# Two of the four weight units of an output projection split earlier, into small tiles

## The chip, the core and the metric

The kernel runs on one core of a Trainium2 chip. The metric is the time of one execution on the device in microseconds (us); three runs of the kernel before gave 1076.39, 1076.57 and 1077.71 us, with a median of 1076.57. One more execution was taken with the hardware profiler, and every row below comes from that one.

## What is computed

One layer of a hybrid block on 528 tokens (16 meta tokens and 512 of the input) of width 1024. The change touches the mixing of the two branches and the projection behind it:

```python
mixed = (jax.nn.sigmoid(ga) * (o_a @ w_branch_rnn[l])
         + jax.nn.sigmoid(gb) * (o_b @ w_branch_ret[l]))
h = h + mixed @ w_out[l]
xn = rms_norm(h, norm_ffn_g[l])
up = causal_dwconv(xn @ w_up[l], ffn_conv_w[l], ffn_conv_b[l])
```

Here `ga` and `gb` are columns of the normed input times `w_in`, `o_a` is the output of the recurrent branch (1280 wide) and `o_b` that of the retention branch (2048 wide). `w_out` is 1024 x 1024. The result is in float32 and the kernel keeps near that precision: each float32 operand is split into two float16 forms, a high one (scaled and rounded) and a low one (the rest), and each product is three matmuls (high by high, high by low, low by high: `SPLIT`).

## The kernel before, in words

**Weights.** All weights come from HBM as float32 in *units* of at most 1 MB, listed once in the order of use (`unit`, line 110; the list is built in lines 114 to 181). `unit_load` (line 186) takes the next unit of the list, claims one of the **two** raw buffers (`wraw`, `bufs=2`, tile `raw`) and issues its load on SP's queue; it returns the unit's *steps*. A step calls `split` (line 90): ScalarE (ACT) makes the high form (line 91), then VectorE (DVE) the low form from the raw data and the high form (line 92). The forms stand in tiles `wt` of the pool `wsp`, ten buffers of 2 x 1024 float16 columns. A raw buffer is free for the next load only when the last low form of its unit is made.

A plain unit has two steps of up to 1024 columns and takes two `wt` tiles. A *fast* unit (`fast_steps`, line 212; a Strassen-like scheme with seven products in place of eight) has five steps and takes four tiles: **cut 1** (512 columns: B11), **cut 2** (1024: B21, B22), three sums on VectorE over the raw data (lines 231 to 233), **cut 3** (1024: T1, T3) and **cut 4** (1024: T4, T2). Cut 3 reads what line 231 writes, cut 4 what lines 232 and 233 write.

**Order.** Steps and loads go strictly in the order of the list. `get(u)` emits all steps up to unit `u`; `tick()` emits one step ahead, as long as the `wt` tiles of the units from the current one to that step's are at most `ahead`. In this part of the program the instructions of each engine are then put into a fixed order when the program is built, by a list scheduler; on the chip each engine runs its own list in that order, and an instruction that waits holds back all that stand behind it.

**The stretch of the change.** Block `i` (`gate_b(i)`, line 1038, i = 0 to 3) makes columns 256 i to 256 i + 255 of the mixed result: a gate unit of `w_in` (*gate unit i*, `u_gb[i]`) and two units of `w_branch_ret` (*branch units 2 i and 2 i + 1*, `u_bb`). Each runs `fast_products` (line 768) on TensorE (PE), here in seven steps: B11 into the bank `pa` (ACT copies it to `kept`), T3 into `pe`, T2 added in `pa` (copied to `kept` again), B21 into `pb`, T1 added in `pa` (copied to `last`), B22 added in `pa` (read by `func`), T4 added in `pe`. `pa` is one PSUM bank, so T2, T1 and B22 can start only when ACT has made the copy ahead of them:

```python
        product(pa, "T2", "F6")
        keep(kept[:, h1], pa)
        yield
        pb = bank("pb")
        product(pb, "B21", "A12", True)
        nc.vector.tensor_tensor(g0[:, h0], pb[:, :257], kept[:, h0], op=ALU.add)
        yield
        product(pa, "T1", "F5")
        keep(last[:, h0], pa)
```

In between, `branch` (line 991, tile `pm`) multiplies the ten tiles `oa` of the first branch with a unit of `w_branch_rnn`; the eighth and last of these stands between blocks 1 and 2. Each `oa` is a *piece*, a buffer of the pool `pieces` (46 buffers, line 57), and is read for the last time there.

After block 3 `out_proj(i)` (line 1104) multiplies the mixed tiles `mx` with the four units of `w_out` (*output units 0 to 3*, `u_out`, line 172, two tiles `wt` each), and after each of its four row tiles come a norm (lines 317 to 331), transposes (line 337, `ptr`) and splits (`x2h`, `x2l`). The last norm runs beside the first three half products of the up projection (line 383).

Of the kernel before, what the change touches and what calls it, by code (L numbers as in the profile page):

```python
# [9 lines left out]
F16 = mybir.dt.float16  # L10
# [4 lines left out]
P = 128  # L15
# [14 lines left out]
SW = 2.0 ** 8  # L30
# [20 lines left out]
def hybrid_block_kernel(ctx, tc, x, meta, norm_mix_g, w_in, conv_w, conv_b, rg_a_w, rg_a_b,  # L51
# [5 lines left out]
    pieces = ctx.enter_context(tc.tile_pool(name="pieces", bufs=46))  # L57
    wraw = ctx.enter_context(tc.tile_pool(name="wraw", bufs=2))
    wsp = ctx.enter_context(tc.tile_pool(name="wsp", bufs=10))
# [24 lines left out]
    def piece(shape, dtype, name):  # L84
        return pieces.tile(shape, dtype, name=name, tag="s")
# [4 lines left out]
    def split(hi, lo, src, s):  # L90
        nc.scalar.activation(hi, src, AF.Copy, scale=s)  # L91
        nc.vector.scalar_tensor_tensor(lo, src, s, hi, op0=ALU.mult, op1=ALU.subtract)  # L92
# [3 lines left out]
    def load(dst, src):  # L96

        if last_load[0] is None:
            last_load[0] = nc.sync.dma_start(dst, src)
        else:  # L100
            with tc.issue_after(last_load[0].ins):
                last_load[0] = nc.sync.dma_start(dst, src)


    def kmaj(w, k0, nk, c0, ncol):
        return w[k0 * P:(k0 + nk) * P, c0:c0 + ncol].rearrange("(k p) c -> p k c", p=P)

    units = []

    def unit(nk, ncol, parts, fast=False):  # L110
        units.append((nk, ncol, parts, fast))
        return len(units) - 1

    o_ur, o_ug, o_q, o_k, o_v, o_gr, o_ga, o_gb = 0, 1280, 2560, 3584, 4608, 6656, 8704, 9728
# [1 line left out]
    for n in range(2):  # L116
        u_ur.append((unit(8, P, [(0, 0, kmaj(w_in, 0, 8, o_ur + P * n, P))]), 0))
    for i in range(1, 5):
        u = unit(8, 256, [(0, 0, kmaj(w_in, 0, 8, o_ur + 256 * i, 256))])
        u_ur += [(u, 0), (u, P)]  # L120
    u_ug = [unit(8, 256, [(0, 0, kmaj(w_in, 0, 8, o_ug + 256 * i, 256))]) for i in range(5)]
    u_q, u_k = [], []
    for h in range(HEADS):
# [21 lines left out]
    def add_ba():  # L145
        u_ba.append(unit(10, P, [(0, 0, kmaj(w_brnn, 0, 10, P * len(u_ba), P))]))

    def add_gate(us, o):
        us.append(unit(8, 256, [(0, 0, kmaj(w_in, 0, 8, o + 256 * len(us), 256))], fast=True))

    def add_bb():
        i = len(u_bb) // 2
        for g in range(2):
            rows = w_bret[8 * P * g:8 * P * (g + 1)].rearrange("(i j p) c -> p j i c", i=4, j=2)
            u_bb.append(unit(8, 256, [(4 * j, 0, rows[:, j, :, 256 * i:256 * i + 256]) for j in range(2)], fast=True))
# [6 lines left out]
    add_gate(u_ga, o_ga)  # L162
    add_ba()
    add_ba()
    for i in range(4):
        add_gate(u_gb, o_gb)
        add_bb()
        if i == 0:
            add_gate(u_ga, o_ga)
        if i < 2:  # L170
            add_ba()
    u_out = [unit(2, 1024, [(0, 0, kmaj(w_out, 2 * a, 2, 0, 1024))]) for a in range(4)]
    u_up = []
    for j in range(12):
        u_up.append([unit(8, 256, [(0, 0, kmaj(w_up, 0, 8, a * DFF + 256 * j, 256))]) for a in range(2)])
# [7 lines left out]
    wviews = []  # L183
    loaded = []

    def unit_load(cuts=1):

        nk, ncol, parts, fast = units[len(loaded)]
        raw = wraw.tile([P, 2048], F32, name="raw")
        n = nk * ncol  # L190
        rv = raw[:, :n].rearrange("p (k c) -> p k c", k=nk)
        for k0, c0, ap in parts:
            load(rv[:, k0:k0 + ap.shape[1], c0:c0 + ap.shape[2]], ap)
        loaded.append(len(loaded))
        if fast:
            return fast_steps(rv, nk // 2, ncol // 2)
        hk = nk // 2
        hn = hk * ncol
        tiles = []

        def step(i, c):
            def run():
                if c == 0:
                    tiles.append(wsp.tile([P, 2, 1024], F16, name="wt"))
                sl = slice(c * hn // cuts, (c + 1) * hn // cuts)
                split(tiles[i][:, 0, sl], tiles[i][:, 1, sl], raw[:, i * hn:(i + 1) * hn][:, sl], SW)
            return run

        wviews.append(lambda a, k, c0, m: tiles[k // hk][:, a, k % hk * ncol + c0:k % hk * ncol + c0 + m])
        return [step(i, c) for i in range(2) for c in range(cuts)]  # L210

    def fast_steps(rv, bk, bc):


        tiles = []
        top, low = slice(0, bk), slice(bk, 2 * bk)
        left, right = slice(0, bc), slice(bc, 2 * bc)

        def cut(rows, cols):
            def run():  # L220
                t = wsp.tile([P, 2, 1024], F16, name="wt")
                src = rv[:, rows, cols]
                n = bk * src.shape[2]
                tv = [t[:, a, :n].rearrange("p (k c) -> p k c", k=bk) for a in range(2)]
                tiles.append(tv)
                split(tv[0], tv[1], src, SW)
            return run

        def sums():
            pair = rv[:, top].rearrange("p k (h c) -> p h k c", h=2)  # L230
            nc.vector.tensor_tensor(pair, pair, rv[:, :, right].rearrange("p (h k) c -> p h k c", h=2), op=ALU.add)  # L231
            nc.vector.tensor_tensor(rv[:, low, right], rv[:, top, left], rv[:, low, right], op=ALU.add)
            nc.vector.tensor_tensor(rv[:, low, left], rv[:, low, left], rv[:, low, right], op=ALU.add)

        at = {"B11": (0, 0), "B21": (1, 0), "B22": (1, bc), "T1": (2, 0), "T3": (2, bc), "T4": (3, 0), "T2": (3, bc)}

        def form(nm, a, k):
            i, c0 = at[nm]
            return tiles[i][a][:, k, c0:c0 + bc]

        wviews.append(form)
        return [cut(top, left), cut(low, slice(0, 2 * bc)), sums,
                cut(top, slice(0, 2 * bc)), cut(low, slice(0, 2 * bc))]
# [4 lines left out]
    current = [0]  # L248

    def unit_tiles(u):  # L250
        return 4 if units[u][3] else 2

    def emit_step():
        u, run = steps[done[0]]
        while len(loaded) < min(u + 2, len(units)):
            queue(unit_load())
        run()
        done[0] += 1
# [4 lines left out]
    def get(u):  # L263
        current[0] = max(current[0], u)
        while len(loaded) <= u:
            queue(unit_load())
        while done[0] < len(steps) and steps[done[0]][0] <= u:
            emit_step()
        return wviews[u]

    def tick(n=1):

        for _ in range(n):
            if done[0] == len(steps):
                if len(loaded) == len(units):
                    return
                queue(unit_load())
            u = steps[done[0]][0]
            if sum(unit_tiles(i) for i in range(current[0], u + 1)) > ahead[0]:
                return  # L280
            emit_step()
# [340 lines left out]
    for n in range(NR):  # L622
        ps = acc("ps")
        u, col = u_ug[n // 2], (n % 2) * P
# [49 lines left out]
    for h in range(HEADS):  # L674
        t = [[piece([P, 2, T], F16, f"qk{h}{i}{m}") for m in range(2)] for i in range(2)]
# [207 lines left out]
    def gate_unit(h, i):  # L883
        ot = oraw[h]

        def finish(j, g):
            nc.vector.tensor_mul(ot[2 * i + j], g[:, :TQ], ot[2 * i + j])
            if j == 0:
                ob_forms(h, i, ot[2 * i], ot[2 * i + 1])

        return fast_products([get(u_gr[h][i])], x_forms, gate_func(AF.Silu), finish)
# [130 lines left out]
    for i in range(2):  # L1022
        run = gate_unit(3, i)
# [48 lines left out]
    wo = [get(u) for u in u_out]  # L1072
# [196 lines left out]
    def combine(pd, left, right):  # L1269

        e1 = work.tile([P, 512], F32, name="e1", tag="w")
        nc.scalar.activation(e1, pd["P1"], AF.Copy)
        yield
        s2 = total(pd["P6"], e1, "s2")
        yield
        s3 = total(pd["P7"], s2, "s3")
        add(1, left, s3, un)
        yield
        add(1, left, pd["P4"], un)
        yield  # L1280
        s7 = total(pd["P5"], s3, "s7")
        add(1, right, s7, -un)
        s4 = total(pd["P5"], s2, "s4")
        add(0, right, s4, -un)
        yield
        add(0, left, e1, un)
        add(0, left, pd["P2"], un)
        yield
        add(0, right, pd["P3"], -un)
        yield  # L1290
# [9 lines left out]
    for q in range(6):  # L1300
        get(u_dn[q])
        run = combine(pd, slice(0, 256), slice(512, 768))
# [22 lines left out]
    run = combine(pd, slice(256, 512), slice(768, 1024))  # L1325
# [78 lines left out]
```

## Time and profile before

| | us |
|---|---|
| median of three runs | 1076.57 |
| the profiled execution | 1076.25 |
| its span, first to last instruction | 1074.5 |
| TensorE busy in the span (matmuls) | 1055.9 (98%) |
| VectorE busy | 839.0 (78%) |
| ScalarE busy | 567.5 (53%) |
| GpSimd busy | 6.8 (1%) |
| 16 DMA engines, HBM read | 108.57 MB |

Times in the rows below count from the span's start. The granted clock of TensorE is at 90% or more in each of the page's 40 slices, 0.999 in the mean. Busy time of TensorE is the union of its matmuls' spans, which overlap: a matmul of 257 columns has a span of 0.27 us, but the next starts 0.11 us later.

### The profile page before, as it was taken

What the parts mean: (1) busy time and instruction counts of PE and PEld (TensorE: products, weight loads), DVE (VectorE), ACT (ScalarE), POOL (GpSimd) and SP (SyncE); (2) the same over time, 40 slices, a digit from 0 to 9 for tenths busy, and PEclk for the clock granted to TensorE, in tenths of its full rate; (3) what the DMA queues carried; (4) which work ended last, traced back from release to release, by engine and by line L of the source; (5) the groups of instructions that cost most, each with busy time, mean ns of one, the idle gap of its engine ahead of it and who ended that gap; (6) DMA issues with size and microseconds to landing.
All of it is one profiled execution on the core that took longest, in us unless ns stands there. A gap on an engine that the chain in (4) does not pass through costs nothing.

```text
span 1074.5 us, 20950 instructions
## 1 busy us (share of the span) xinstructions
PE 1055.9 (98%) x9037; PEld 855.1 (80%) x9037; DVE 839.0 (78%) x1219; ACT 567.5 (53%) x847; POOL 6.8 (1%) x20
## 2 busy tenths in 40 slices
PE   8999999999999999999999999999999999999997
PEld 5888888865684858888888885588888888888885
DVE  6875799998786969878697785578767777888875
ACT  6558954435564747566454453365444544454442
POOL 2000000000000000000000000000000000000000
PEclk9999999999999999999999999999999999999999
DMA  7432243431212212423333355143232323113322
GB/s 220 133 117 80 80 138 119 157 120 40 80 41 72 88 62 65 128 89 119 103 104 119 118 200 174 38 159 118 79 118 80 119 79 118 41 60 126 111 79 79
DMA packets 108027, 112.00 MB, mean 104 GB/s; under 512 B 5546, under 2 KB 99472, under 8 KB 107936
## 3 DMA queue, kind: packets, MB, share of 16 engines
q1 hardware_dynamic: 107504, 110.27, 31.4%
q8 instruction: 70, 1.15, 0.4%
q10 hardware_dynamic: 144, 0.26, 0.1%
q0 software_dynamic: 288, 0.14, 0.1%
q14 instruction: 21, 0.17, 0.0%
HBM read 108.57 MB, written 2.10 MB: 103 GB/s over the span
## 4 chain that ended last, share of the span: by engine, by line
PE 75%; DVE 14%; ACT 8%; issue 2%; DMA 1%; SPq 0%; ACTq 0%; DVEq 0%
PE ps L370 33%; PE P L1240 9%; PE pa L776 9%; PE ps L839 4%; PE pm L370 4%; PE ps L1112 4%; PE pe L776 4%; DVE wt L92 3%; PE ps L383 3%; PE pb L776 2%; ACT wt L91 2%; PE ps L861 1%; DVE rnn L575 1%; DVE raw L231 1%; ACT L627 1%
## 5 line engine op out<-in xcount | busy, mean ns | idle before, releaser
L370 PEld LDWEIGHTS <-wt 128*128 128x128 f16 x4224 | 410.5, 97 | 63.7 <-DVE t L667 1.4
L92 DVE SCALAR_TENSOR_TENSOR wt<-raw,wt 128x1024 f16<-128x1024 f32 (+2 forms) x270 | 296.6, 1111 | 71.5 <-ACT wt L91 69.5
L91 ACT ACTIVATE wt<-raw 128x1024 f16<-128x1024 f32 (+2 forms) x270 | 256.4, 965 | 161.1 <-PE ps L370 28.3
L776 PEld LDWEIGHTS <-wt 128*128 128x128 f16 x2016 | 195.0, 97 | 36.0 <-issue 8.8
L370 PE MATMUL ps<-x2h,wt 128*128 128x258 f16 x1440 | 218.8, 273 | 0.0
L370 PE MATMUL ps<-xh,wt 128*128 128x257 f16 (+2 forms) x1056 | 163.8, 275 | 1.1 <-DVE t L667 1.1
L370 PE MATMUL ps<-x2l,wt 128*128 128x258 f16 x720 | 137.7, 272 | 0.0
L1197 DVE SCALAR_TENSOR_TENSOR cv<-ps,vt,cv 128x512 f32<-128x512 f32 x96 | 71.9, 749 | 54.7 <-ACT cv L1195 53.4
L370 PE MATMUL ps<-xl,wt 128*128 128x257 f16 (+2 forms) x528 | 102.2, 275 | 0.0
L1240 PE MATMUL P<-wt,act 128*128 128x256 f16 x792 | 88.3, 273 | 0.0
L1240 PEld LDWEIGHTS <-act 128*128 128x128 f16 x792 | 77.5, 98 | 9.0
L839 PE MATMUL ps<-wt,xh 128*128 128x512 f16 x256 | 76.4, 379 | 1.2 <-DVE v L92 1.0
L776 PE MATMUL pa<-xs,wt 128*128 128x257 f16 x576 | 71.6, 273 | 4.8 <-ACT kept L781 4.5
L1195 ACT ACTIVATE cv<-ps,vt,vt 128x512 f32<-128x512 f32 x48 | 37.1, 773 | 56.8 <-PE ps L370 52.2
L370 PE MATMUL pm<-oa,wt 128*128 128x257 f16 x480 | 55.4, 274 | 0.0
L839 PEld LDWEIGHTS <-xh 128*128 128x128 f16 x256 | 24.8, 98 | 30.9 <-issue 2.9
L839 PE MATMUL ps<-wt,xl 128*128 128x512 f16 x128 | 48.5, 379 | 0.0
L776 PE MATMUL pa<-ob,wt 128*128 128x257 f16 x384 | 45.7, 274 | 0.6 <-ACT last L781 0.5
L1112 PE MATMUL ps<-wt,mx 128*128 128x512 f16 x192 | 44.3, 379 | 0.0
L231 DVE TENSOR_TENSOR raw<-raw 128x1024 f32<-128x1024 f32 x35 | 42.7, 1220 | 0.6
L1112 PEld LDWEIGHTS <-mx 128*128 128x128 f16 x192 | 17.6, 98 | 18.5
L861 PE MATMUL ps<-sc,v 128*128 128x257 f16 (+4 forms) x384 | 32.1, 236 | 0.0
(250 smaller groups left out, 1273.5 us busy)
## 6 DMA issues: line engine op xcount, KB each, us to landing
raw<-in_w_in SPq DMA_DIRECT2D x41, 1024.0 KB, 4.8
raw<-in_w_up SPq DMA_DIRECT2D x24, 1024.0 KB, 5.0
raw<-in_w_down SPq DMA_DIRECT2D x48, 256.0 KB, 3.4
raw<-in_w_branch_ret SPq DMA_DIRECT2D x16, 512.0 KB, 4.3
raw<-in_w_branch_rnn SPq DMA_DIRECT2D x8, 640.0 KB, 4.2
raw<-in_w_out SPq DMA_DIRECT2D x4, 1024.0 KB, 4.9
xin<-in_x SPq DMA_DIRECT2D x4, 512.0 KB, 4.9
h<-in_x SPq DMA_DIRECT2D x4, 512.0 KB, 4.3
```

What stands on the lines that cost most here:

```text
L91: nc.scalar.activation(hi, src, AF.Copy, scale=s)
L92: nc.vector.scalar_tensor_tensor(lo, src, s, hi, op0=ALU.mult, op1=ALU.subtract)
L231: nc.vector.tensor_tensor(pair, pair, rv[:, :, right].rearrange("p (h k) c -> p h k c", h=2), op=ALU.add)
L370: nc.tensor.matmul(ps[:, hf, :n], w(aw, k, col, P), src(ax, k, c0, n), start=k == 0 and (aw, ax) == (0, 0), stop=k == nk - 1 and aw == 1)
L383: mm = nc.tensor.matmul(ps[:, hf, :n], w(aw, k, col, P), src(ax, k, c0, n), start=k == 0 and (aw, ax) == (0, 0), stop=k == KD - 1 and aw == 1)
L776: nc.tensor.matmul(ps[:, :257], ws[k // 4](wf, aw, k % 4), src(xf_, ax, k), start=first and k == 0 and (aw, ax) == (0, 0), stop=k == last_ ...
L839: nc.tensor.matmul(pb, xf(ax, k, XF + j0, nb), w(aw, k % 4, 0, 512), start=i == 0, stop=i == 23)
L861: nc.tensor.matmul(ps[:, hf, s0 - lo_i:257], vt[b][:, va, d * P:(d + 1) * P], st[SCP[b][0]][:, sa, o:o + hi_i - s0], start=i == 0, stop=i ...
L1112: nc.tensor.matmul(ps[:, n], mx[k][:, a, c0:c0 + P], wo[k // 2](aw, k % 2, n * 512, 512), start=k == 0 and (a, aw) == (0, 0), stop=k == ks ...
L1195: nc.scalar.activation(vv_, ps[:, :, 2:258], AF.Identity, scale=vt2[:, 96 + ch:97 + ch], bias=b_ff[:, ch:ch + 1])
L1197: nc.vector.scalar_tensor_tensor(vv_, ps[:, :, j:j + 256], vt2[:, 48 * j + ch:48 * j + ch + 1], vv_, op0=ALU.mult, op1=ALU.add)
L1240: nc.tensor.matmul(pd[:, 256 * tt:256 * tt + 256], t[:, ax, c0 + tt * P:c0 + tt * P + P], w(wf, aw, i), start=q % 6 == 0 and tt == 0 and i ...
```

## The change

The output units 0 and 1 move forward in the list of units: before, all four stood behind the last branch unit; now output unit 0 stands behind branch unit 3 and the last unit of `w_branch_rnn`, and output unit 1 behind branch unit 5. These two don't use `wt` tiles. Each makes its forms in four pieces `wo` of 2 x 512 columns from the pool `pieces`, in two steps of two splits each, and counts with no tile against `ahead`. Output units 2 and 3 are as before. A view (`wviews`) finds the piece by row block and column; the matmuls are the same.

```diff
-    def unit(nk, ncol, parts, fast=False):
-        units.append((nk, ncol, parts, fast))
+    def unit(nk, ncol, parts, fast=False, where="wsp"):
+        units.append((nk, ncol, parts, fast, where))
...
+    u_out = []
+
+    def add_out():
+        a = len(u_out)
+        u_out.append(unit(2, 1024, [(0, 0, kmaj(w_out, 2 * a, 2, 0, 1024))], where="pieces" if a < 2 else "wsp"))
+
     for i in range(4):
         add_gate(u_gb, o_gb)
         add_bb()
...
         if i < 2:
             add_ba()
-    u_out = [unit(2, 1024, [(0, 0, kmaj(w_out, 2 * a, 2, 0, 1024))]) for a in range(4)]
+        if i in (1, 2):
+            add_out()
+    add_out()
+    add_out()
...
+        def piece_step(i):
+            def run():
+                for j in (2 * i, 2 * i + 1):
+                    t = piece([P, 2, 512], F16, "wo")
+                    tiles.append(t)
+                    split(t[:, 0], t[:, 1], raw[:, 512 * j:512 * j + 512], SW)
+            return run
+
+        if where == "pieces":
+            wviews.append(lambda a, k, c0, m: tiles[(k * ncol + c0) // 512][:, a, c0 % 512:c0 % 512 + m])
+            return [piece_step(i) for i in range(n // 1024)]
...
     def unit_tiles(u):
-        return 4 if units[u][3] else 2
+        return 0 if units[u][4] == "pieces" else 4 if units[u][3] else 2
```

**On SP's queue.** The loads from the last unit of `w_branch_rnn` on, before (an `in_w_in` load is a gate unit, a pair of `in_w_branch_ret` loads a branch unit, `in_w_out` an output unit):

```order
L102 DMA raw_6794<-in_w_branch_rnn 128x10x128
L102 DMA raw_6841<-in_w_in 128x8x256
L102 DMA raw_7072<-in_w_branch_ret 128x4x256 x2
L102 DMA raw_7110<-in_w_branch_ret 128x4x256 x2
L102 DMA raw_7210<-in_w_in 128x8x256
L102 DMA raw_7257<-in_w_branch_ret 128x4x256 x2
L102 DMA raw_7455<-in_w_branch_ret 128x4x256 x2
L102 DMA raw_7555<-in_w_out 128x2x1024
```

and now:

```order
L102 DMA raw_6794<-in_w_branch_rnn 128x10x128
L102 DMA raw_6841<-in_w_out 128x2x1024
L102 DMA raw_6874<-in_w_in 128x8x256
L102 DMA raw_7086<-in_w_branch_ret 128x4x256 x2
L102 DMA raw_7124<-in_w_branch_ret 128x4x256 x2
L102 DMA raw_7224<-in_w_out 128x2x1024
L102 DMA raw_7271<-in_w_in 128x8x256
L102 DMA raw_7310<-in_w_branch_ret 128x4x256 x2
L102 DMA raw_7483<-in_w_branch_ret 128x4x256 x2
```

Output unit 0 has moved ahead of gate unit 2 and its two branch units, and output unit 1 ahead of gate unit 3 and its two. With two raw buffers each load waits for the last low form of the unit two places ahead of it, or of the one whose buffer comes free first.

**On ScalarE, around the start of block 2.** From cut 1 of branch unit 4 to the copy of block 2's B11 (`kept`), before:

```order
L91 ACTIVATE wt_7113<-raw_7072 128x512
L91 ACTIVATE wt_7129<-raw_7072 128x1024
L91 ACTIVATE wt_7162<-raw_7072 128x1024
L91 ACTIVATE mx_6978<-m_5795 128x514
L91 ACTIVATE wt_7179<-raw_7072 128x1024
L91 ACTIVATE mx_7008<-m_5663 128x514
L91 ACTIVATE wt_7212<-raw_7110 128x512
L91 ACTIVATE wt_7215<-raw_7110 128x1024
L781 ACTIVATE kept_7092<-pa_7096 128x257
```

and now, where line 802 is line 781 of before:

```order
L91 ACTIVATE wt_7127<-raw_7086 128x512
L91 ACTIVATE wo_6879<-raw_6841 128x512
L91 ACTIVATE wo_6882<-raw_6841 128x512
L91 ACTIVATE wt_7143<-raw_7086 128x1024
L91 ACTIVATE wo_6885<-raw_6841 128x512
L91 ACTIVATE mx_6992<-m_5795 128x514
L91 ACTIVATE mx_7022<-m_5663 128x514
L91 ACTIVATE wt_7176<-raw_7086 128x1024
L802 ACTIVATE kept_7106<-pa_7110 128x257
L91 ACTIVATE wt_7193<-raw_7086 128x1024
L802 ACTIVATE kept_7106<-pa_7110 128x257
```

Three of output unit 0's four pieces stand here; in the program they wait for the last reads of `oa` tiles by the eighth `pm` product. All cuts of branch unit 4 and two of branch unit 5 stood ahead of the copy; now cuts 1 to 3 of unit 4 do, cut 4 stands between the first copy and the second, and those of unit 5 behind.

**On ScalarE, in block 3's gate part.** Up to the copy `last` ahead of its B22, before:

```order
L91 ACTIVATE mx_7404<-m_6138 128x514
L91 ACTIVATE wt_7557<-raw_7455 128x512
L91 ACTIVATE wt_7560<-raw_7455 128x1024
L781 ACTIVATE kept_7437<-pa_7441 128x257 x2
L91 ACTIVATE mx_7434<-m_6069 128x514
L781 ACTIVATE last_7438<-pa_7441 128x257
```

and now (`raw_7310` is branch unit 6, `raw_7483` branch unit 7):

```order
L91 ACTIVATE mx_7432<-m_6138 128x514
L802 ACTIVATE kept_7465<-pa_7469 128x257
L91 ACTIVATE wt_7535<-raw_7310 128x1024
L802 ACTIVATE kept_7465<-pa_7469 128x257
L91 ACTIVATE mx_7462<-m_6069 128x514
L91 ACTIVATE wt_7552<-raw_7310 128x1024
L91 ACTIVATE wt_7585<-raw_7483 128x512
L91 ACTIVATE wt_7588<-raw_7483 128x1024
L802 ACTIVATE last_7466<-pa_7469 128x257
```

Cuts 3 and 4 of branch unit 6 and cuts 1 and 2 of branch unit 7 now stand between the copies; before, unit 6 was done by then and unit 7's cuts 1 and 2 stood ahead of the first copy.

## Rows read from the trace of the kernel before

**Rows 1.** The page's busy times: engine, us, share of the span, instructions.
```profile
PE 1055.9 (98%) x9037; PEld 855.1 (80%) x9037; DVE 839.0 (78%) x1219; ACT 567.5 (53%) x847; POOL 6.8 (1%) x20
```
**Rows 2.** TensorE's waits from 560 to 720: total us, times, longest.
```profile
PE ptr L337 <- DVE xo L330: 0.6, 1, 0.6
PE pa L776 <- ACT kept L781: 0.5, 1, 0.5
PE pa L776 <- ACT last L781: 0.5, 1, 0.5
```
**Rows 3.** Timeline of SP's queue: start, us, issue (two answers).
```profile
567.78 0.37 SPq L102 DMA_DIRECT2D raw<-in_w_in  x1
570.14 0.92 SPq L102 DMA_DIRECT2D raw<-in_w_branch_ret  x2
...
584.20 0.92 SPq L102 DMA_DIRECT2D raw<-in_w_branch_ret  x2
...
594.44 0.37 SPq L102 DMA_DIRECT2D raw<-in_w_in  x1
```
**Rows 4.** DMA issues at 567.78, 584.20 and 626.5: KB, us to landing.
```profile
raw<-in_w_in SPq DMA_DIRECT2D x1, 1024.0 KB, 5.0
raw<-in_w_branch_ret SPq DMA_DIRECT2D x2, 512.0 KB, 3.9
h<-in_x SPq DMA_DIRECT2D x2, 512.0 KB, 5.3
```
**Rows 5.** Timeline of VectorE: start, us, what [idle before].
```profile
582.95 1.82 DVE L92 SCALAR_TENSOR_TENSOR wt<-raw,wt 128x1024 f16<-128x1024 f32 x2
...
592.54 0.69 DVE L92 SCALAR_TENSOR_TENSOR mx<-m,mx 128x514 f16<-128x514 f32 x1
593.15 1.82 DVE L92 SCALAR_TENSOR_TENSOR wt<-raw,wt 128x1024 f16<-128x1024 f32 x2
...
595.49 1.22 DVE L92 SCALAR_TENSOR_TENSOR wt<-raw,wt 128x1024 f16<-128x1024 f32 x1
596.62 1.22 DVE L231 TENSOR_TENSOR raw<-raw 128x1024 f32<-128x1024 f32 x1
```
**Rows 6.** Timeline of ScalarE.
```profile
572.83 1.58 ACT L91 ACTIVATE wt<-raw 128x512 f16<-128x512 f32 x2 [1.71 <-DMA raw<-in_w_in]
...
594.85 0.39 ACT L781 ACTIVATE kept<-pa 128x257 f32<-128x257 f32 x1 [0.22 <-PE pa L776]
597.93 1.06 ACT L91 ACTIVATE wt<-raw 128x1024 f16<-128x1024 f32 x1 [2.69 <-DVE raw L231]
598.89 0.37 ACT L781 ACTIVATE kept<-pa 128x257 f32<-128x257 f32 x1
```
**Rows 7.** Timeline of TensorE, last `pm` product and block 2's gate part.
```profile
587.07 6.42 PE L370 MATMUL pm<-oa,wt 128*128 128x257 f16 x56
...
594.65 1.49 PE L776 MATMUL pe<-xs,wt 128*128 128x257 f16 x12
595.98 1.49 PE L776 MATMUL pa<-xs,wt 128*128 128x257 f16 x12
...
599.31 1.49 PE L776 MATMUL pa<-xs,wt 128*128 128x257 f16 x12 [0.51 <-ACT kept L781]
```
**Rows 8.** Timeline of TensorE, block 3: T1 and B22 of both parts.
```profile
627.65 1.49 PE L776 MATMUL pa<-xs,wt 128*128 128x257 f16 x12
628.98 0.61 PE L776 MATMUL pa<-ob,wt 128*128 128x257 f16 x4
629.68 1.49 PE L776 MATMUL pa<-xs,wt 128*128 128x257 f16 x12
...
645.76 2.82 PE L776 MATMUL pa<-ob,wt 128*128 128x257 f16 x24 [0.47 <-ACT last L781]
```
**Rows 9.** Timeline of VectorE and TensorE in the last norm before the up projection.
```profile
702.61 1.21 DVE L92 SCALAR_TENSOR_TENSOR wt<-raw,wt 128x1024 f16<-128x1024 f32 x1
...
704.62 0.63 PE L337 MATMUL ptr<-ident,xo 128*128 128x128 f32 x4 [0.65 <-DVE xo L330]
```

More of the change, by code (lines that the diff above doesn't have):

```diff
@@ L186, in unit_load @@
     def unit_load(cuts=1):
-        nk, ncol, parts, fast = units[len(loaded)]
+        nk, ncol, parts, fast, where = units[len(loaded)]
         raw = wraw.tile([P, 2048], F32, name="raw")
```

## Prediction

> **What bounds the kernel now.** I read the page first: TensorE is busy for 1055.9 of 1074.5 us [rows 1], so time can be won only in its gaps, and is lost wherever a new gap opens; VectorE (78%) and ScalarE matter by when they finish, not by how much they do. Then TensorE's waits in the stretch of the change, 560 to 720: three, of 0.5, 0.5 and 0.6 us, 1.6 us together [rows 2]. That is all this change can win by moving work. The first two are copies out of the bank `pa` that came late because ScalarE stood at a weight form: at 597.93 it had waited 2.69 us for VectorE's sum, made the form, and copied only at 598.89 [rows 6], so T1 began at 599.31 after 0.51 idle [rows 7]. The third is the last norm, whose second vector step began only when a weight form was done [rows 9]. Last I read SP's queue for the loads and the three engines' timelines for durations.
>
> **What the change costs in work: nothing on the path.** TensorE runs the same matmuls over the same columns. Eight splits of 512 columns replace four of 1024: on VectorE the next instruction begins 0.61 us after one of 514 columns and 1.13 us after one of 1024 [rows 5], so 8 x 0.61 less 4 x 1.13 is 0.4 us more; on ScalarE a 512 and a 1024 form together take 1.58 and the 1024 alone 1.06 [rows 6], so 8 x 0.52 less 4 x 1.06 is nothing. Both engines have idle time for that [rows 1].
>
> **What it moves: the loads.** There are two raw buffers. Before, gate unit 2's load went out at 567.78 and its first form began at 572.83 [rows 3, 6]. Now output unit 0 takes that buffer, and gate unit 2 the one that comes free at 570.1 (branch unit 4's load went out there before [rows 3]): 2.4 us later, landing at 575.1 after 5.0 us [rows 4], long before it is needed. But output unit 0 keeps its buffer: its pieces 2 to 4 wait for the last `pm` product, which resumes at 587.07 [rows 7]. So gate unit 2 and branch unit 4 share one buffer. Branch unit 4 can load only when gate unit 2's last low form is done, 584.1 by [rows 5], at the place of the pair issued at 584.20 [rows 3]; it lands 3.9 us later [rows 4], at 588.1. Before, it had been there ten microseconds.
>
> **Term 1, block 2: +0.8 us.** From 588.1 ScalarE makes cut 1 (0.6) and the second piece (0.6), to 589.3. VectorE then has, in its order: two low pieces, an addition, cut 1's low form, a low piece, two low forms of `mx` (seven of 0.61, 4.3), cut 2's low form (1.13) and the sum of line 231 (1.14): 595.8. Only then can ScalarE make cut 3 (1.06), and the copy of B11 stands behind cut 3: 595.9 + 1.05 + 0.3 gives 597.25. T2, which began at 595.98 [rows 7], waits until then: +1.3. The second copy stands behind cut 4, ready at 598.8 (an addition, the sum of line 232, cut 3's low form, the sum of line 233: 2.95), so it ends at 600.15 and T1 begins at 600.2 in place of 599.31 [rows 7]: the old wait of 0.51 is partly paid, and 0.9 remains, of which the filler behind it takes back 0.1. Nearest bounds: 0 if the sums are done when B11 is (594.85 [rows 6]); 2.7 if the landing takes the 5.3 us that loads take in company [rows 4] (1.4 more). I take 3.9, the row of the same kind of load at the same event.
>
> **Term 2, block 3's gate part: +1.8 us.** Branch unit 5 loads when the fourth piece's low form is done, at 592.4 (before: 584.20 [rows 3]), in time for its products by 0.8 and 1.8 us. Its cut 4 is done at 609.2, and only then does gate unit 3 load, at 594.44 before [rows 3]. It lands at 614.0; VectorE, done with output unit 1 at 610.9, idles 3.7 us and then has gate unit 3, branch units 6 and 7 and block 2's end to do without a pause to 638. By the same counting the sum for branch unit 6's cut 3 is done at 627.35, and ScalarE makes cut 3 before the second copy of gate unit 3's products: T1 begins at 628.8 in place of 628.45 (its old 627.65 [rows 8] plus 0.8), +0.4. Then cut 4 of unit 6 (sum at 629.75) and cuts 1 and 2 of unit 7 stand before `last`: 629.85 + 1.0 + 0.55 + 0.95 + 0.3 gives 632.65. B22 then follows T1 by 3.9 us, before by 2.03 [rows 8]; four more filler matmuls (0.11 each) are pulled forward: +1.4. Bounds: 0 if VectorE has caught up, 3.5 if gate unit 3's landing is 1.5 us later.
>
> **Term 3, block 3's second part: +1.2 us.** Branch unit 7's T3 is ready 0.2 us late. The copy `last` at the end now stands behind the up projection's first cut, whose load can go only when output unit 2's forms are made, at 642.7; landed at 647.7 and cast by 649.1, it lets `last` end at 649.4, where T1 ended at 647.95: a wait of 1.5 us in place of 0.47 [rows 8], +1.0. Bounds 0 and 3 (a landing 1.5 us later, as before).
>
> **Term 4, the last norm: -0.65 us.** With six `wt` tiles free beside output units 2 and 3, four of the first up units' cuts are made before the norms, and no weight form stands on ScalarE between the square and the root there or on VectorE between the reciprocal and the product. The step that began at 703.73, after 702.61 + 1.1, moves forward by more than the wait of 0.65 [rows 9]; that is gone, its upper bound. Next late would be nothing that the rows show.
>
> The sum is 0.8 + 1.8 + 1.2 - 0.65 = 3.15 us on the profiled 1076.25, so 1079.4; the median lies 0.3 above the profiled execution, so **1079.7 us**.
>
> The Trainium skill ("SBUF — State Buffer", The DMA setup-cost knee) puts a load at about 2 us plus its bytes at 436 GB/s, 4.4 us for 1 MB and 3.2 for half of one. Rows 4 show 5.0 and 3.9, so the trace speaks against the page by 0.6 us; by the page's figures terms 1 to 3 would each be about 0.5 smaller and the sum near 1.7 us.
>
> **Rivals.** *Faster or level, chance 0.16.* The forms made ahead empty ScalarE and VectorE where TensorE waits, and the three waits of 1.6 us go: 1076.57 - 1.6 = 1075.0. For it: VectorE is idle for 22% of the span [rows 1], and the pieces need no `wt` tile. Against it: two of the three waits come from a copy queued behind a form, and the new order queues more copies so. The Trainium skill ("Perfetto Trace Analysis", Optimizing Scalar/DVE Operations) says that where these engines aren't saturated but make others wait, breaking up instructions may let work be done sooner. By that rule this rival is what comes; no row of before has such pieces, so none bears it out.
>
> *Lateness absorbed, not slower, chance 0.24.* Gate unit 2's first form began at 572.83 [rows 6] and its T3 ran at 594.65 [rows 7], so weights stood ready far ahead, and loads 2 to 15 us later may still do if landings are quick. The mechanism is one copy: if line 231's sum for branch unit 4 is done by 594.8, term 1 vanishes, and a unit that is 1 us earlier takes most of terms 2 and 3. The point is a landing below about 3 us at 584.2 in place of 3.9, or VectorE's list shorter by one form. Left is 0.3 to 1.5 of new waits less 0.65: 1076.3 to 1077.4.
>
> *A cascade, chance 0.12.* Each load waits for the last form of the unit before it, so a wait of TensorE at one unit delays the buffer of the next. If landings take 5.3 us [rows 4] along the five loads of branch units 4 to 7 and gate unit 3, about 1.4 us is added at three places: 1079.7 + 4 = 1083.7.
>
> That the change doesn't do what it says is not left open: the order shows the pieces ahead and the tiles free.
>
> **How the numbers follow.** The forecast has 0.48: +1.5 to +5.0 us, 1078 to 1081.5. A measurement of this kernel can tell about 0.2% (2.15 us) from no change, so 1074.4 to 1078.7 is "same". Of the forecast 0.40 lies above and 0.08 inside; of the first rival 0.04 is faster by more than 0.2% and 0.12 inside; of the second 0.22 inside and 0.02 above; the cascade is above. Faster 0.04, same 0.42, slower 0.54. The range leaves out the lower half of the first rival and the upper half of the cascade: 1075.2 to 1083.2.
>
> **What would show it.** In the changed profile: branch unit 4's loads issued about 584 and its first form after 588 (right) or near 583 (wrong); gate unit 3's load after 605 in place of 594; TensorE waits on `kept` and `last` of 4 to 5 us in total between 595 and 650 in place of 1.0; none on `xo` near 705. If the waits on the copies stay at 1 us while the loads are as late, my counting of VectorE's list is wrong; if the loads aren't late, the holding of the buffer is. A time below 1076 makes the whole argument wrong.

## The result and the profile after

The changed kernel takes 1081.91 us (median of 6 runs, 1080.74 to 1083.45), the kernel before 1076.67 beside it: a ratio of 1.0048, 95% interval 1.0037 to 1.006, **5.2 us slower**. The profiled execution took 1080.74 us (span 1078.9), the shortest of the six and 4.5 above the profiled execution of before. In the order of the rows of before:

The page's busy times answer to [rows 1]; all of the work is there again, in a longer span.
```profile
PE 1056.4 (98%) x9037; PEld 855.1 (79%) x9037; DVE 839.5 (78%) x1223; ACT 567.7 (53%) x851; POOL 6.8 (1%) x20
```
TensorE's waits from 560 to 725 us (total, times, longest) answer to [rows 2]. They are 5.5 us in place of 1.6: the wait on `xo` has gone, and all that is left are copies out of the bank `pa`.
```profile
PE pa L797 <- ACT last L802: 3.9, 2, 2.4
PE pa L797 <- ACT kept L802: 1.6, 3, 1.0
```
SP's queue answers to [rows 3]. Output unit 0 now loads first; the four issues from 584.52 are branch units 4 and 5 (before: 570.14 and 584.20), 609.52 is gate unit 3 (594.44), 640.92 output unit 3, and the first of the four at 643.19 is up unit 0. This trace is 0.32 us later than that of before when the stretch begins (568.10, 567.78). The view of waits counts from the end of the last matmul's span, 0.27 us, while the next would have begun after 0.11, so each wait costs about 0.16 us more than it shows: 3.9 us more in two waits more, and the 0.32, are the 4.5 between the two profiled executions.
```profile
568.10 0.37 SPq L102 DMA_DIRECT2D raw<-in_w_out  x1
...
584.52 9.02 SPq L102 DMA_DIRECT2D raw<-in_w_branch_ret  x4
...
609.52 0.37 SPq L102 DMA_DIRECT2D raw<-in_w_in  x1
...
640.92 0.38 SPq L102 DMA_DIRECT2D raw<-in_w_out  x1
643.19 16.16 SPq L102 DMA_DIRECT2D raw<-in_w_up  x4
```
ScalarE answers to [rows 6]. Each copy (`kept`, `last`) follows a cut (`wt<-raw`) that has waited: for VectorE's sum at 596.11, for up unit 0's load at 649.78.
```profile
588.31 0.63 ACT L91 ACTIVATE wt<-raw 128x512 f16<-128x512 f32 x1 [5.34 <-DMA raw<-in_w_branch_ret]
...
596.11 1.06 ACT L91 ACTIVATE wt<-raw 128x1024 f16<-128x1024 f32 x1 [3.62 <-DVE raw L252]
597.07 0.37 ACT L802 ACTIVATE kept<-pa 128x257 f32<-128x257 f32 x1
...
645.89 2.00 ACT L91 ACTIVATE wt<-raw 128x1024 f16<-128x1024 f32 x2 [2.01 <-DMA raw<-in_w_out]
649.78 1.06 ACT L91 ACTIVATE wt<-raw 128x1024 f16<-128x1024 f32 x1 [1.88 <-DMA raw<-in_w_up]
650.74 0.37 ACT L802 ACTIVATE last<-pa 128x257 f32<-128x257 f32 x1
```
TensorE answers to [rows 7, 8]: the products that waited.
```profile
597.49 1.49 PE L797 MATMUL pa<-xs,wt 128*128 128x257 f16 x12 [1.03 <-ACT kept L802]
...
600.50 1.49 PE L797 MATMUL pa<-xs,wt 128*128 128x257 f16 x12 [0.19 <-ACT kept L802]
...
629.40 1.49 PE L797 MATMUL pa<-xs,wt 128*128 128x257 f16 x12 [0.41 <-ACT kept L802]
...
633.27 1.49 PE L797 MATMUL pa<-xs,wt 128*128 128x257 f16 x12 [1.50 <-ACT last L802]
...
651.16 2.82 PE L797 MATMUL pa<-ob,wt 128*128 128x257 f16 x24 [2.40 <-ACT last L802]
```

### The profile page after: what moved, and what is told of

It is laid out like the page before. It is cut to its first block, busy times and chain, and to the rows that moved or that the text cites. A ratio compares the mean times of both kernels' runs of the same rounds, so it can differ in the third digit from the quotient of the medians.

```text
span 1078.9 us, 20941 instructions
## 1 busy us (share of the span) xinstructions
PE 1056.4 (98%) x9037; PEld 855.1 (79%) x9037; DVE 839.5 (78%) x1223; ACT 567.7 (53%) x851; POOL 6.8 (1%) x20
## 4 chain that ended last, share of the span: by engine, by line
PE 71%; DVE 16%; ACT 8%; DMA 2%; issue 2%; SPq 1%; ACTq 0%; DVEq 0%
PE ps L391 33%; PE P L1261 9%; PE pa L797 6%; PE ps L860 4%; DVE wt L92 4%; PE pm L391 4%; PE ps L1133 4%; PE ps L404 3%; PE pe L797 3%; ACT wt L91 2%; PE pb L797 2%; DVE raw L252 1%; PE ps L882 1%; DVE rnn L596 1%; DMA raw<-in_w_in 1%
## 5 line engine op out<-in xcount | busy, mean ns | idle before, releaser
L391 PEld LDWEIGHTS <-wt 128*128 128x128 f16 x4224 | 410.5, 97 | 63.7 <-DVE t L688 1.4
L92 DVE SCALAR_TENSOR_TENSOR wt<-raw,wt 128x1024 f16<-128x1024 f32 (+2 forms) x266 | 291.7, 1109 | 68.0 <-ACT wt L91 65.7
L91 ACT ACTIVATE wt<-raw 128x1024 f16<-128x1024 f32 (+2 forms) x266 | 251.8, 963 | 166.2 <-PE ps L391 28.3
L797 PEld LDWEIGHTS <-wt 128*128 128x128 f16 x2016 | 195.0, 97 | 41.1 <-issue 13.6
L404 PEld LDWEIGHTS <-wt 128*128 128x128 f16 x288 | 27.9, 97 | 4.8 <-issue 0.3
```

Source lines behind the costliest of these rows:

```text
L391: nc.tensor.matmul(ps[:, hf, :n], w(aw, k, col, P), src(ax, k, c0, n), start=k == 0 and (aw, ax) == (0, 0), stop=k == nk - 1 and aw == 1)
L404: mm = nc.tensor.matmul(ps[:, hf, :n], w(aw, k, col, P), src(ax, k, c0, n), start=k == 0 and (aw, ax) == (0, 0), stop=k == KD - 1 and aw == 1)
L797: nc.tensor.matmul(ps[:, :257], ws[k // 4](wf, aw, k % 4), src(xf_, ax, k), start=first and k == 0 and (aw, ax) == (0, 0), stop=k == last_ ...
```

## The experiments

The theory to start with was the prediction's: the held buffer and a further unit in a stream of two buffers make loads late, and copies stand behind cuts that wait for them. Its rivals: the small cuts themselves cost; the order in ScalarE's queue alone costs, whatever the loads do; the late loads cost even where the queue is right. Here are all runs; "waits" are TensorE's from 560 to 725 us in the profiled execution, by the sums of that view.

| run | us, median | ratio to before, 95% interval | waits, us |
|---|---|---|---|
| before | 1076.4 to 1076.7 | | 1.6 |
| changed | 1081.91 | 1.0048 (1.0037 to 1.006) | 5.5 |
| 1 up unit 0's cut behind `last` | 1078.51 | 1.002 (1.0011 to 1.0029) | 3.9 |
| 2 output unit 0 alone moved | 1077.76 | 1.0015 (1.0006 to 1.0023) | 2.3 |
| 3 one unit alone, at the second place | 1077.85 | 1.0012 (1.0003 to 1.0021) | 2.9 |
| 4 pieces at the old place | 1077.39 | 1.0006 (0.9997 to 1.0015) | 2.1 |
| 5 changed, again | 1082.66 | 1.0051 (1.0038 to 1.0063) | 5.4 |
| 6 two loads more, no pieces | 1076.84 | 1.0004 (0.9996 to 1.0013) | 1.8 |
| 7 pieces at the old place, copies first | 1074.83 | 0.9981 (0.9972 to 0.999) | 0.5 |
| 8 changed, copies first | 1079.44 | 1.003 (1.002 to 1.004) | 4.9 |
| 9 before, one edge | 1075.63 | 0.9993 (0.9984 to 1.0002) | 1.1 |
| 10 changed, all cuts behind the copies | 1077.12 | 1.0009 (1.0 to 1.0018) | 2.3 |
| 11 as 7, again | 1074.84 | 0.9985 (0.9976 to 0.9994) | 0.5 |

**Run 1. One edge in the changed kernel.** `keep` hands back its instruction, and up unit 0's cuts are traced under an edge to it.
```diff
-        run()
+        if u == u_up[0][0]:
+            with tc.issue_after(lastcopy[0]):
+                run()
+        else:
+            run()
```


> The changed kernel with one edge more: ScalarE's first cut of up unit 0 stands behind the copy of `last` of the third branch block, and nothing else moves. Theory (loads late, and the copy queued behind a cut that waits for a late load): the wait of TensorE on `last`, 2.40 us in the changed kernel, falls to about 0.5 us (0.47 in the kernel before), the other waits (1.0, 0.4, 1.5 us) stay, and the time falls by 1.9 us, from 1081.9 to about 1080.0. Rival (the copy is late for its own product or for VectorE, or the 1.9 us come back as a wait in the output projection): the time stays at 1081.9.

1078.51 us. The first cut of up unit 0 now follows `last`, and the wait of 2.40 is 0.47; the other four waits stayed (1.2, 0.2, 0.5, 1.5). ScalarE of this run:
```profile
645.66 2.00 ACT L91 ACTIVATE wt<-raw 128x1024 f16<-128x1024 f32 x2 [1.94 <-DMA raw<-in_w_out]
648.63 0.39 ACT L807 ACTIVATE last<-pa 128x257 f32<-128x257 f32 x1 [0.97 <-PE pa L802]
649.64 2.00 ACT L91 ACTIVATE wt<-raw 128x1024 f16<-128x1024 f32 x2 [0.62 <-DMA raw<-in_w_up]
```
So the theory holds for this term, but 3.4 us went from median to median where it had 1.9. The two profiled executions differ by 2.2 (1080.74, 1078.56); run 5 shows a part of the rest.

**Runs 2 and 3. One unit alone.** The other three stand behind the last branch unit, in the old form.
```diff
-        if i in (1, 2):
+        if i == 1:
```
(run 3: `i == 2`; both with `where="pieces" if a < 1`)

> Only output unit 0 is moved, and is made in pieces; units 1 to 3 stay behind the last branch unit. Theory (the held buffer makes branch unit 4 late; the second 1 MB in the two-buffer stream makes gate unit 3 late): TensorE's waits in the second branch block are those of the changed kernel (1.0 and 0.2 us), gate unit 3 is loaded near 601 us and not 609, so the waits of the third block's gate part are under 0.6 us in sum and not 1.9, and the time is 1077.0 to 1078.5 us. Rival (every moved unit costs the same by its small cuts on ScalarE and VectorE): half of the 5.2 us, 1079.3.

> Only one output unit is moved, to the second place of the change (behind branch unit 5), and is made in pieces; the other three stay behind the last branch unit. Theory: the second branch block is as before (one wait of 0.5 us), gate unit 3 is loaded after 605 us as in the changed kernel, and the third block's gate part waits 1.5 to 2.5 us; with the `last` of the third block late by 0.5 to 2 us the time is 1078.5 to 1081 us. Rival (the held buffer of unit 0 starts the whole delay, and a unit whose pieces are free at once costs nothing): 1076.0 to 1077.0, with no wait over 0.6 us.

1077.76 and 1077.85 us. Run 2 is what the theory said: TensorE waits 1.01 and 0.19 in block 2, gate unit 3 loads at 601.23, and block 3's gate part waits for nothing. Run 3 is under the theory's 1078.5 to 1081: gate unit 3 loaded at 604.22, not after 605, and its lateness cost one wait of 0.61. What cost 0.76 is something else, which ScalarE shows: four pieces, all free and all loaded, in front of `last`.
```profile
599.53 2.19 ACT L91 ACTIVATE wo<-raw 128x512 f16<-128x512 f32 x4 [0.23 <-DMA raw<-in_w_out]
601.63 0.36 ACT L802 ACTIVATE last<-pa 128x257 f32<-128x257 f32 x1
```
By the sums of both, 1.2 + 1.3, the changed kernel would be 2.5 us slower, less the `xo` wait of 0.65 that only both together remove: 1.9, and run 1 stands at 2.0. These are not the same waits, though: run 3's 0.76 stands in block 2, and the 1.50 of block 3 in neither run, so the sum is no proof that the two costs add. The rest, 3.2, goes with up unit 0's cut, which stands ahead of that `last` in neither.

**Run 4. The pieces at their old place.**
```diff
-        if i in (1, 2):
-            add_out()
-    add_out()
-    add_out()
+    for _ in range(4):
+        add_out()
```


> Output units 0 and 1 are made in pieces, eight 512-column cuts for four cuts of 1024, but at their old place behind the last branch unit: no load before them moves. Theory (the loads cost, the small cuts do not): the waits before 625 us are those of the kernel before (0.51), `last` waits 0.5 or less, the wait of 0.65 us on `xo` is gone since four tiles more are free: 1075.0 to 1076.7 us. Rival (the small cuts on ScalarE and VectorE cost): the copies of the third branch block come late, `last` waits over 1.5 us, 1078 us or more.

1077.39 us, no clear difference from before, and neither theory's picture. The `xo` wait is gone, but `kept` of the third branch block waits 1.10: four pieces of output unit 1, late by their load, stand ahead of it. ScalarE:
```profile
641.76 2.19 ACT L91 ACTIVATE wo<-raw 128x512 f16<-128x512 f32 x4 [4.99 <-DMA raw<-in_w_out]
643.86 0.36 ACT L800 ACTIVATE kept<-pa 128x257 f32<-128x257 f32 x1
```
No load before the last branch unit moved here, and yet a copy waits. That made the queue's order the better suspect.

**Run 5. The changed kernel again.** No edit.

> The changed kernel once more, unaltered, for a second profile and more times. Theory (the load of up unit 0 ends last before the third branch block's `last`, so its landing time goes into the kernel's time one for one): the runs spread over 2 us or more around 1081.9, and the profiled run's time is 1078.3 us plus its own wait on `last` of the third block (1080.74 with 2.40 us in the first profile). Rival (the spread comes from elsewhere): that wait is 2.4 us again whatever the time is, and other waits or the granted clock account for the difference.

The rival is right: this profiled execution took 1082.75 us, 2.0 more than the first, with the same wait, 2.42. TensorE around it:
```profile
651.48 4.47 PE L797 MATMUL pa<-ob,wt 128*128 128x257 f16 x24 [2.42 <-ACT last L802]
655.78 2.82 PE L797 MATMUL pe<-ob,wt 128*128 128x257 f16 x24
```
The product behind the wait took 4.47 us; in the first profile 2.82. The granted clock says why. Stretches (us, TensorE's busy time and matmuls, granted clock, DMA share, GB/s) of this run, then of the first profile:
```profile
648.81:651.48 2.67, 0.25 (x4) 1.00 0.26 68
652.00:654.00 2.00, 2.00 (x11) 0.50 1.01 359
654.00:656.00 2.00, 2.00 (x15) 0.73 0.41 105
656.00:660.00 4.00, 4.00 (x32) 1.00 0.62 215
```
```profile
648.76:651.16 2.40, 0.00 (x2) 1.00 0.28 50
652.00:654.00 2.00, 2.00 (x20) 1.00 0.95 337
654.00:656.00 2.00, 2.00 (x20) 1.00 0.60 154
656.00:660.00 4.00, 4.00 (x23) 1.00 0.53 189
```
After TensorE had stood for 2.4 us the clock was at half (1.2 GHz) from 652 to 654 in one execution and full (2.4 GHz) in the other. From the start of that product to the start of the next is 4.30 us here and 2.65 there: 1.65 us. That product itself began 0.32 us later here (651.48, 651.16), and the two together are the 2.0. Of run 1's 3.4 us the clock is then a part; how large a part these two profiles don't settle.

**Run 6. Loads without pieces.** Two 1 MB loads at the change's places, from which nothing is made.
```diff
+        if where == "load":
+            return [lambda: nc.gpsimd.tensor_copy(small.tile([P, 1], F32, name="ss"), raw[:, 0:1])]
```


> The kernel before, with two loads more: 1 MB of the output projection's weight is loaded into a raw buffer at each of the change's two places, and GpSimd reads one column of it, which frees the buffer as soon as the load has landed; nothing is made of it, and all four output units stand behind the last branch unit as before. Theory (block 2 is late by the holding of the buffer, block 3 by the place that the second load takes in the two-buffer stream): branch unit 4 is loaded before 577 us and not at 584, the second block waits 0.5 us as before; gate unit 3 is loaded after 605 us, the third block's gate part waits 1.0 to 2.0 us, and the time is 1077.5 to 1078.5 us. Rival (a further transfer is enough to make block 2 late too): the waits of 1.0 and 0.2 us of the changed kernel are in block 2, and the time is over 1078.5.

1076.84 us, no difference that can be told. SP's queue shows branch unit 4 at 573.02 (11 us earlier than in the changed kernel) and gate unit 3 at 600.44 (6 us later than before), and block 3 waits for neither:
```profile
567.63 0.37 SPq L102 DMA_DIRECT2D raw<-in_w_out  x1
...
573.02 11.95 SPq L102 DMA_DIRECT2D raw<-in_w_branch_ret  x4
...
600.44 0.37 SPq L102 DMA_DIRECT2D raw<-in_w_in  x1
```
```profile
PE ptr L362 <- DVE xo L355: 0.7, 1, 0.7
PE pa L801 <- ACT kept L806: 0.6, 1, 0.6
PE pa L801 <- ACT last L806: 0.5, 1, 0.5
```
So a further megabyte in a two-buffer stream costs nothing that can be told, and the price that I expected for block 3 here was wrong. The late load of branch unit 4 comes from the buffer that is held (584.30 in run 2, with that unit alone). Gate unit 3's comes from both units: it is at 601.23 in run 2, 604.22 in run 3, and 609.52 with both.

**Run 7, and 11 for a second measurement. Pieces at the old place, copies first.** Run 4 with edges: `copies` holds the copies of `keep` in order, and a cut is traced only when its copy is.
```diff
+    def behind(u):
+        if u == u_bb[5] and done[0] > 0 and steps[done[0] - 3:done[0]][0][0] == u:
+            return 50
+        return 59 if u == u_out[1] else 60 if u_out[1] < u <= u_up[0][0] else 0
...
+        if behind(u):
+            with tc.issue_after(copies[behind(u) - 1]):
+                run()
```


> Pieces at the old place, and edges that put four cuts behind TensorE's next copy in ScalarE's queue: the third cut of branch unit 5 behind the second `kept` of gate block 2, output unit 1's behind the second `kept` of the third branch block, those of output units 2, 3 and of up unit 0 behind its `last`. Theory (what TensorE waits for in all these kernels is a copy that stands behind a cut): the waits of 0.5 and 1.1 us on `kept` and 0.47 on `last` go, that on `xo` stays away: 1077.4 less 2.1, 1075.0 to 1075.8 us, below the 1076.5 of the kernel before. Rival (the cuts are needed so soon that TensorE waits for the forms instead, on `wt`): 1076.5 to 1077.5.

> Pieces at the old place with copies first, as in the seventh run, again beside the tenth on one chip: 1074.6 to 1075.2 us, 0.1% to 0.2% under the kernel before.

1074.83 and 1074.84 us: **faster than both kernels**, 0.9981 (0.9972 to 0.999) and 0.9985 (0.9976 to 0.9994) of the time before. One wait is left, the `last` whose product B22 directly follows in the same bank:
```profile
PE pa L805 <- ACT last L810: 0.5, 1, 0.5
```
Run 11's profiled execution was the longest of its eleven, 1076.56 us, with the same one wait in this stretch. What made it longer lies at the kernel's start: TensorE idled for 2.30 us there, and behind it the granted clock (third from the right) was at half from 12 to 14 us. At 567.59 this trace was 1.62 us behind run 7's (565.97).
```profile
9.36 1.23 PE L441 MATMUL ptr<-ident,xn 128*128 128x128 f32 x8 [2.30 <-DVE xn L432]
12.00:14.00 2.00, 2.00 (x10) 0.50 1.05 391
```

**Run 8. The changed kernel, copies first.** The loads are as late as before; only ScalarE's order differs.
```diff
+    def behind(u):
+        k = sum(v == u for v, _ in steps[:done[0]])
+        return {(u_bb[4], 3): 49, (u_bb[4], 4): 50, (u_bb[6], 3): 56, (u_bb[6], 4): 57, (u_bb[7], 0): 57,
+                (u_bb[7], 1): 57, (u_up[0][0], 0): 60, (u_up[0][0], 1): 60}.get((u, k), 0)
```


> The changed kernel with its loads and pieces where they are, and edges in ScalarE's queue alone: the cuts that stand ahead of a copy that TensorE waits for (third and fourth of branch unit 4, third and fourth of branch unit 6, first and second of branch unit 7, both of up unit 0) are put behind that copy. Theory Q (late loads cost only through the queue: the copy stands behind a cut whose form nobody needs yet): the waits of 1.0, 0.2, 0.4, 1.5 and 2.4 us shrink to some 0.5 us in sum of the last one's 0.47, no wait on the forms comes up, and the time is 1074.5 to 1076.0 us, under the kernel before. Theory L (the late loads themselves cost): as the copies come in time TensorE waits for the forms instead, on the products of the second and third branch blocks (`wt` or its split), 2 us or more in sum, and the time is 1077.5 us or more; branch unit 7's first form is the one most likely to be late.

1079.44 us: neither. The waits on `kept` are gone, but the cuts of output unit 3 moved up into the place of up unit 0's and held `last` just as long:
```profile
647.24 2.00 ACT L91 ACTIVATE wt<-raw 128x1024 f16<-128x1024 f32 x2 [4.54 <-DMA raw<-in_w_out]
649.14 0.37 ACT L812 ACTIVATE last<-pa 128x257 f32<-128x257 f32 x1
```
```profile
600.93 1.49 PE L807 MATMUL pa<-xs,wt 128*128 128x257 f16 x12 [0.49 <-ACT last L812]
...
617.31 2.82 PE L807 MATMUL pa<-ob,wt 128*128 128x257 f16 x24 [0.33 <-ACT last L812]
...
631.72 0.27 PE L807 MATMUL pe<-xh,wt 128*128 128x257 f16 x1 [0.58 <-DVE g L833]
...
637.32 1.27 PE L807 MATMUL pe<-ob,wt 128*128 128x257 f16 x10 [0.58 <-DVE wt L92]
...
641.00 1.27 PE L807 MATMUL pa<-ob,wt 128*128 128x257 f16 x10 [0.20 <-DVE wt L92]
...
649.56 2.82 PE L807 MATMUL pa<-ob,wt 128*128 128x257 f16 x24 [2.65 <-ACT last L812]
```

**Run 9. One edge in the kernel before.**
```diff
+        return 50 if (u, k) == (u_bb[5], 3) else 0
```


> The kernel before with one edge: the third cut of branch unit 5 stands behind the second `kept` of gate block 2 in ScalarE's queue, a swap of two neighbours. Theory Q: the wait of 0.51 us at 599.31 us goes, the two others (0.47 and 0.65) stay, and the time falls by 0.5 us to about 1076.0. Rival: the swap moves the wait to the form, 1076.5.

1075.63 us. The wait of 0.51 in [rows 7] is gone and the two others are there; the interval, 0.9984 to 1.0002, just reaches 1, so the time alone doesn't settle it.
```profile
PE ptr L346 <- DVE xo L339: 0.6, 1, 0.6
PE pa L785 <- ACT last L790: 0.5, 1, 0.5
```

**Run 10. Output unit 3's cuts behind `last` as well.**
```diff
-                (u_bb[7], 1): 57, (u_up[0][0], 0): 60, (u_up[0][0], 1): 60}.get((u, k), 0)
+                (u_bb[7], 1): 57, (u_out[3], 0): 60, (u_out[3], 1): 60, (u_up[0][0], 0): 60, (u_up[0][0], 1): 60}.get((u, k), 0)
```


> The kernel of the eighth run (moved loads, pieces, copies ahead of cuts) with output unit 3's two cuts behind the third branch block's `last` as well: there they took the place of up unit 0's, waited for their own late load and held `last` for 2.65 us. Theory (both halves are real: most of the 5.2 us are copies queued behind cuts that wait for late loads, and some 2 us are the late forms themselves, which the queue cannot mend): `last` waits 0.5 us, 2.2 us less than there; the waits of 0.5 to 0.6 us on forms and VectorE stay, about 2.2 us in sum with the last-but-one copies; 1076.7 to 1077.3 us, 2 us above the pieces at their old place with copies first (1074.83), and no clear difference from the kernel before. Rival Q (the queue is all of it): 1075.5 us or less. Rival L (out of the queue, the late loads of output unit 3 and up unit 0 are waited for by the output projection and the up products): 1078.5 us or more.

1077.12 us, in the theory's range. With every load as late as in the changed kernel, 4.5 of the 5.2 us are gone by the order of one queue. What stays are forms that come late (`wt` twice, and a sum of VectorE behind the late units' splits) and two shorter waits on `last` (0.17 and 0.28) before its own 0.47; those two copies still stand behind other cuts:
```profile
PE pa L807 <- ACT last L812: 0.9, 3, 0.5
PE pe L807 <- DVE g L833: 0.6, 1, 0.6
PE pe L807 <- DVE wt L92: 0.6, 1, 0.6
PE pa L807 <- DVE wt L92: 0.2, 1, 0.2
```

**What follows.** Against the kernel before: +5.2 as it is (+6.2 in run 5), +2.0 without the cut of up unit 0 ahead of `last`, +0.7 with the other cuts behind their copies too. So 3.2 us go with one copy behind one cut. Of these 1.9 is its waiting. The clock that falls after it in some executions is a part of the rest: five of the changed kernel's eleven have a mean granted clock of 0.996 or 0.997 and took 1082.24 to 1083.45 us. But four have 0.999 and took 1080.74 to 1081.94, and what spreads these is not shown. Then 1.3 are the copies of blocks 2 and 3 behind theirs, and 0.7 is about what the late forms leave once the `xo` wait is off. With the loads at their old place (run 7) pieces and order together are worth 1.6; run 9's one edge has 0.8 of that without pieces, though not clear of noise, and the rest is about the `xo` wait. More of run 7's edges without the pieces were not tried. Each of these steps but the first is about as large as its interval; that the waits go and come with the edges is what carries them. What in VectorE's order leaves run 10's three waits on forms was not tried.

## Why the prediction was right, and where it was not

The forecast was 1079.7 us in 1075.2 to 1083.2, slower; 1081.91 was measured, on that side and in the range. By its steps:

- **The work** was free: run 4 makes every small cut and differs by 0.9 us, 1.1 of which is one copy's place in the queue.
- **The loads** went as counted: branch unit 4 issued at 584.52 and first cut at 588.31 (584.1 and 588.1 forecast, in a trace that is 0.3 late), gate unit 3 at 609.52 (609.2).
- **Term 1**, +0.8: T2 and T1 began at 597.49 and 600.50 (597.25 and 600.2), waits of 1.03 and 0.19 in place of 0.51. Right.
- **Term 2**, +1.8: waits of 0.41 and 1.50, T1 at 629.40 and B22 3.87 us behind it (628.8 and 3.9). Right.
- **Term 3**, +1.2, was mis-sized. I let up unit 0's load go at 642.7 and land in 5.0 us [rows 4]. It went at 643.19, and its cut began at 649.78, 6.6 later, with output unit 3's megabyte issued 2.3 us ahead of it. The wait was 2.40 in place of 1.5: 0.9 too little.
- **Term 4**, -0.65: right, no wait on `xo`.
- **"The median lies 0.3 above the profiled execution"** failed. It lies 1.2 above here, in part since the profile fell on an execution in which the clock stayed full behind the 2.40 us; the sum had a price for waiting and none for the clock. It was also the shortest of all eleven executions, which is chance. Term 3's 0.9, this 0.9 and the 0.3 by which the trace was late ahead of the stretch are nearly all of the 2.2 us between forecast and result.

What the runs put beside the forecast is the cause. I had the loads first and the queue second. The lateness is real, but 4.5 of the 5.2 us were paid through the place of five copies in ScalarE's queue, where cuts stood in front, most of which nobody needed yet. The row was there: the wait of 0.51 in [rows 6, 7] was such a copy, and run 9 takes it away with a swap of two instructions. Rival one, faster at 1075.0, did not come with this change; run 7 reached 1074.83, but by the order, and by two of the same three waits: the `last` of 0.47 stayed. By the 0.16 us that each wait hides, the three that the prediction has at 1.6 are about 2.1. The Trainium skill ("Perfetto Trace Analysis", Optimizing Scalar/DVE Operations) has it that breaking up instructions may let work be done sooner: in run 4 broken-up work alone gave nothing that can be told, and with the copies ahead of it 1.6 us, half of which run 9's median has without breaking anything up.

## What to carry to other kernels

On an in-order engine look, for each copy that the bound engine waits for, at what stands in front of it: a step that waits for a late load but whose result is needed only later belongs behind the copy. Here edges that say so took back 4.5 us with every load as late as it was. When work is moved ahead, ask which buffer it holds while it waits, and what a scheduler will then put into the gap. Where a new wait of some microseconds opens on TensorE, price the clock behind it too, and look at two profiles.

## What the runs showed of the hardware

The same kernel with the same wait of 2.4 us came back once at full clock and once at 1.2 GHz for the next product, 1.65 us apart (rows of run 5); run 8's profile stayed at full clock behind 2.65 us, and no kernel whose waits were 1.5 us or less showed a fall between 595 and 660. The one other fall ahead of the last matmuls is that at the start of run 11's profile, behind 2.30 us; the other twelve profiles idle there for 0.34 to 1.89 us and stay at full clock. The kernel before has longer executions too: of the 92 taken beside the runs 12 took 1077.92 to 1078.57 us, all at a mean granted clock of 0.997, and the others at most 1076.93. So not every fall comes from this change. What decides one these runs don't show.

The other lateness that I had not expected is the landing: a megabyte that took 5.0 us on its own row [rows 4] took 6.6, issue to cut, when another had been issued 2.3 us ahead. For the one ahead it is open: output unit 3's, with up unit 0's issued 2.3 us behind it, took 6.3 in run 8 (640.97 to 647.24) and 5.0 in the changed kernel (640.92 to 645.89). The Trainium skill ("SBUF — State Buffer", The DMA setup-cost knee) has a fit from which an estimate for 1 MB is about 4.4 us. The measured values here are all above it.
